# An FFN's operand rewritten with norm and shift from the third pair of tiles on, rows begun 64 bytes past 128, and a first modulation in five rounds

## The chip, the cores and the metric

The kernel runs on one core of a Trainium2 chip, as one launch. The metric is the device time of that launch in microseconds (us). All arithmetic is in float32; a product of two float32 operands is built from three matmuls in the rounded format float32r (the high parts with each other, and each high part with the other operand's low part).

## The reference

One step of a small diffusion backbone over 384 tokens of width 1024: 128 context tokens and 256 latent ones. There are two layers; each is half an FFN, a token mixer (latent attention, MLA, in layer 0; a state space model, SSM, in layer 1), and half an FFN.

```python
def adaln_input(x, g, shift, scale):
    return rmsnorm(x, g) * (1 + scale) + shift

def swiglu(h, w_in, w_out):
    gate, up = jnp.split(h @ w_in, 2, axis=-1)
    return (jax.nn.silu(gate) * up) @ w_out

def ffn_half(x, shift, scale, gate, g, w_in, w_out):
    return x + 0.5 * gate * swiglu(adaln_input(x, g, shift, scale), w_in, w_out)
```

Shift, scale and gate come from `silu(cond) @ mod_w + mod_b`, one set for context tokens and one for latent ones. `w_in` is 1024 x 5632, `w_out` 2816 x 1024. Every mixer, too, reads a normed and modulated x.

## The kernel before

Channels lie on the 128 partitions and tokens along the free axis. x is kept as `xT`, 8 rows of 384 tokens. The matmul operand is `xh` (high part) and `xl` (low part): x times scale and weight of the norm (`gs`), with two more columns, 384 and 385, that hold the shift of the two token groups. So a row has `NX` = 386 columns. The factor of the norm (one number per token) is not in it: it is found while the first matmuls run, spread over all partitions into `rext`, and multiplied into each result on its way out of PSUM, where the shift's column is added as a bias.

`wmm` takes the next 128 x 128 weight tile from a stream. Weights arrive as units of 8 tiles (512 KB) by `stream_dma`, four ahead; `stream_split` cuts a unit into `whi` (ScalarE, L109) and `wlo` (VectorE, L110), three ahead; a unit that is used up starts the split of the third next. Each `wmm` is three matmuls (L124, L125, L126: xh with wlo, xl with whi, xh with whi).

An FFN's first half computes 44 tiles of 128 outputs over 8 rows k: 22 pairs of a gate tile j and an up tile 22 + j, 1056 matmuls ("in" in the trace). `evac` turns a pair into the product, `ah` and `al`. The second half ("fo") multiplies these 22 rows with `w_out`, 8 tiles, 528 matmuls; `residual` adds each to x, writes the next operand's row (`prep_x`) and its square. `in_first_pair` starts the FFNs, MLA and SSM: 7 rows of two tiles, the norm's statistic (`norm_stat`) between them, and then row 7, which is written last. `Fill` spreads the modulation of later stages, VectorE sums over weight rows, over the matmuls of an FFN.

The first FFN has a head of its own, since its shift and scale must first be computed: in four rounds (`mod_round`), each of which gives two rows k. A round is a load of 2 MB in four pieces, 8 matmuls that sum over 1024 channels in four column groups (`psmod`, L141; the trace has two instructions for each), a copy, transposes, a reduction, and the rows of `xh` and `xl`. Between the rounds six tiles (`HEAD` = 3 pairs) take the rows that are ready.

The order of instructions on each engine is that of a list scheduler: what comes first in the program goes first, but an instruction that is not ready by the scheduler's own model of time lets later ones pass. Tiles of a pool lie one behind the other in the order in which they are first named, each begun on a multiple of 32 bytes.

## Time and profile before

| what | value |
|---|---|
| time, median of 3 runs | 1695.97 us (1695.53 to 1696.38) |
| profiled execution: time, span | 1695.77 us, 1694.0 us |
| busy: TensorE, VectorE, ScalarE, GpSimd | 1655.4, 1254.1, 791.7, 196.1 us |
| HBM traffic | 276.06 MB read, 4.28 MB written |

The span runs from the first instruction of the program to the last; the time has a little more around it. The profile calls TensorE's matmuls PE, its weight loads PEld, VectorE DVE, ScalarE ACT, GpSimd POOL, and the engine that issues most loads SP (SPq is its queue). Matmuls are pipelined: one begins before the one ahead has ended, so the time that one takes of the engine is the distance between starts and not its duration.

### The profile page before, as it was taken

What the parts mean: (1) busy time and instruction counts of PE and PEld (TensorE: products, weight loads), DVE (VectorE), ACT (ScalarE), POOL (GpSimd) and SP (SyncE); (2) the same over time, 40 slices, a digit from 0 to 9 for tenths busy, and PEclk for the clock granted to TensorE, in tenths of its full rate; (3) what the DMA queues carried; (4) which work ended last, traced back from release to release, by engine and by line L of the source; (5) the groups of instructions that cost most, each with busy time, mean ns of one, the idle gap of its engine ahead of it and who ended that gap; (6) DMA issues with size and microseconds to landing.
All of it is one profiled execution on the core that took longest, in us unless ns stands there. A gap on an engine that the chain in (4) does not pass through costs nothing.

```text
span 1694.0 us, 25203 instructions
## 1 busy us (share of the span) xinstructions
PE 1655.4 (98%) x9616; PEld 1584.6 (94%) x9631; DVE 1254.1 (74%) x2069; ACT 791.7 (47%) x1308; POOL 196.1 (12%) x180
## 2 busy tenths in 40 slices
PE   7999999999999999999999999999998999999996
PEld 3899999987899999999999999988897999999996
DVE  3798889579868888986888897888876765444443
ACT  3533333455544333334333333787766644333332
POOL 0111100110001111000111100023222201111000
PEclk9999999999999999999999999999998999999998
DMA  9476667443245666664666574354433333333331
GB/s 349 172 228 210 206 203 235 131 151 101 75 164 183 204 206 202 214 229 157 208 205 205 193 241 164 121 166 134 141 122 119 97 125 123 125 125 125 124 125 50
DMA packets 88441, 281.99 MB, mean 166 GB/s; under 512 B 9836, under 2 KB 19900, under 8 KB 87808
## 3 DMA queue, kind: packets, MB, share of 16 engines
q1 hardware_dynamic: 86560, 274.26, 49.6%
q0 software_dynamic: 1104, 5.28, 0.9%
q8 instruction: 75, 1.23, 0.3%
q10 hardware_dynamic: 656, 0.85, 0.1%
q14 instruction: 46, 0.38, 0.1%
HBM read 276.06 MB, written 4.28 MB: 165 GB/s over the span
## 4 chain that ended last, share of the span: by engine, by line
PE 88%; DVE 5%; ACT 4%; DMA 2%; issue 1%; SPq 0%; POOL 0%; DVEq 0%; ACTq 0%
PE in L124 17%; PE in L126 17%; PE in L125 17%; PE fo L124 7%; PE fo L126 7%; PE fo L125 7%; DVE ca L662 2%; DMA cp<-ecum_d 2%; PE so L124 1%; PE so L125 1%; PE so L126 1%; ACT L769 1%; PE psmod L141 1%; PE wo L124 1%; PE pv L548 1%
## 5 line engine op out<-in xcount | busy, mean ns | idle before, releaser
L124 PE MATMUL in<-xh,wlo 128*128 128x386 f32 x1792 | 613.0, 343 | 3.6 <-ACT xh L246 3.1
L109 ACT CAST whi<-raw 128x1024 fp32r<-128x1024 f32 x348 | 365.3, 1050 | 526.2 <-issue 227.0
L126 PE MATMUL in<-xh,whi 128*128 128x386 f32 x1792 | 610.1, 341 | 0.0
L125 PE MATMUL in<-xl,whi 128*128 128x386 f32 x1792 | 608.3, 339 | 0.2 <-DVE xl L248 0.2
L110 DVE TENSOR_TENSOR wlo<-raw,whi 128x1024 fp32r<-128x1024 f32 x348 | 430.5, 1237 | 129.9 <-ACT whi L109 129.6
L124 PEld LDWEIGHTS in<-xh,wlo 128*128 128x128 f32 x1792 | 339.2, 189 | 10.6 <-issue 4.5
L125 PEld LDWEIGHTS in<-xl,whi 128*128 128x128 f32 x1792 | 339.8, 190 | 4.9 <-issue 2.4
L126 PEld LDWEIGHTS in<-xh,whi 128*128 128x128 f32 x1792 | 337.9, 189 | 3.7 <-issue 3.7
L125 PE MATMUL fo<-al,whi 128*128 128x384 f32 x704 | 236.7, 336 | 0.0
L124 PE MATMUL fo<-ah,wlo 128*128 128x384 f32 x704 | 236.7, 336 | 0.0
L126 PE MATMUL fo<-ah,whi 128*128 128x384 f32 x704 | 236.7, 336 | 0.0
L183 DVE CUSTOM_DVE_ANT_0 work<-modraw,crow,cst 128x1024 f32<-128x1024 f32 x144 | 185.3, 1288 | 20.6 <-POOL al L327 19.3
L327 POOL TENSOR_TENSOR al<-work,ah 128x384 fp32r<-128x384 f32 x88 | 111.2, 1263 | 749.6 <-ACT ah L326 736.2
L124 PEld LDWEIGHTS fo<-ah,wlo 128*128 128x128 f32 x704 | 132.0, 187 | 0.0
L125 PEld LDWEIGHTS fo<-al,whi 128*128 128x128 f32 x704 | 132.0, 187 | 0.0
L126 PEld LDWEIGHTS fo<-ah,whi 128*128 128x128 f32 x704 | 132.0, 187 | 0.0
L183 DVE CUSTOM_DVE_ANT_0 workout<-modraw,crow,cst 128x1024 f32<-128x1024 f32 x96 | 123.1, 1282 | 6.5 <-DMA modraw<-in_modw_dram 5.0
L326 ACT CAST ah<-work 128x384 fp32r<-128x384 f32 x88 | 45.3, 514 | 131.0 <-DVE work L324 131.0
L319 DVE TENSOR_TENSOR work<-in,rext 128x386 f32<-128x386 f32 x88 | 49.1, 558 | 69.7 <-PE in L126 67.8
L320 DVE TENSOR_TENSOR work<-in,rext 128x386 f32<-128x386 f32 x88 | 48.8, 554 | 45.3 <-PE in L126 45.3
L322 ACT ACTIVATE work<-work 128x128 f32<-128x128 f32 (+1 forms) x176 | 70.6, 447 | 4.5 <-DVE work L319 4.1
L324 DVE SCALAR_TENSOR_TENSOR work<-work 128x128 f32<-128x128 f32 (+1 forms) x176 | 68.0, 427 | 5.2
(257 smaller groups left out, 1683.4 us busy)
## 6 DMA issues: line engine op xcount, KB each, us to landing
raw<-in_w_dram SPq DMA_DIRECT2D x348, 512.0 KB, 3.8
modraw<-in_modw_dram SPq DMA_DIRECT2D x128, 512.0 KB, 4.4
mod<-in_mod_dram SPq DMA_DIRECT2D x16, 512.0 KB, 9.9
cp<-ecum_d SPq DMA_DIRECT2D x32, 256.0 KB, 5.0
crow<-silu_d POOLq DMA_DIRECT2D x4, 1024.0 KB, 6.1
h<-in_h_dram SPq DMA_DIRECT2D x16, 128.0 KB, 3.4
out_dram<-sto SPq DMA_DIRECT2D x16, 128.0 KB, 2.3
xT<-in_xT_dram SPq DMA_DIRECT2D x4, 384.0 KB, 9.3
```

The lines of the kernel that those rows point to most:

```text
L109: nc.scalar.copy(his[u], raws[u])
L110: tt(out=los[u], in0=raws[u], in1=his[u], op=ALU.subtract)
L124: mm(out, wl, rh, start=start, stop=False)
L125: mm(out, wh, rl, start=False, stop=False)
L126: mm(out, wh, rh, start=False, stop=stop)
L183: nc.vector.tensor_tensor_reduce(out=junk(), in0=raw[n], in1=crow[:, s, :], scale=1.0, scalar=C("modb", j), op0=ALU.mult, op1=ALU.add, acc ...
L319: tt(out=g, in0=pg[:, :NX], in1=rext, op=ALU.mult)
L320: tt(out=u, in0=pu[:, :NX], in1=rext, op=ALU.mult)
L322: act(sg[:, a:b], g[:, a:b], AF.Silu, bias=g[:, NTOK + s:NTOK + s + 1])
L324: stt(out=sg[:, a:b], in0=u[:, a:b], scalar=u[:, NTOK + s:NTOK + s + 1], op0=ALU.add, in1=sg[:, a:b], op1=ALU.mult)
L326: nc.scalar.copy(ah[:, j, :], sg)
L327: nc.gpsimd.tensor_tensor(out=al[:, j, :], in0=sg, in1=ah[:, j, :], op=ALU.subtract)
```

## The change

There are four parts.

- **Operand written anew.** The first pairs of an FFN (two of them in `first_four`, three in the head of the first FFN) run as before on 386 columns, but row by row over all their tiles. Once `rext` is there, `normed_x` rewrites each row of `xh` and `xl` in place: t = x times gs times rext, xh = t + shift rounded, xl = t + shift - xh. From the third pair (in the first FFN the fourth) on, tiles read 384 columns, and `evac` is one Silu and one multiply. MLA and SSM keep the old way.
- **Rows.** A row of `xh` and `xl` is 416 floats apart (13 x 128 bytes), and `gs`, `pad`, `sel` and `rs` are placed or sized so that these rows, those of `ah` and `al` and MLA's operands begin 64 bytes past a multiple of 128.
- **Five rounds.** The first modulation comes in rounds of 1, 1, 2, 2 and 2 rows; all but the first round are loaded by one DMA each. Their places between head matmuls are written out anew.
- **Ahead of the first sums.** A Silu on a zeroed tile ahead of the constants' arrival, and five matmuls on zeros ahead of and between the sums of the first round.

```diff
+XROW = 416
+ROUNDS = ((0, 1), (1, 1), (2, 2), (4, 2), (6, 2))
...
+    gs = pers.tile([P, KT, 2], F32, tag="gs", name="gs")
+    xh = pers.tile([P, KT, XROW], F32R, tag="xh", name="xh")[:, :, 0:NX]
+    xl = pers.tile([P, KT, XROW], F32R, tag="xl", name="xl")[:, :, 0:NX]
-    xh = pers.tile([P, KT, NX], F32R, tag="xh", name="xh")
-    xl = pers.tile([P, KT, NX], F32R, tag="xl", name="xl")
+    rext = pers.tile([P, XROW], F32, tag="rext", name="rext")[:, 0:NX]
...
+    class FirstMod:
+        def __init__(self, pool, c32):
+            self.pool, self.c32, self.raw, self.sb = pool, c32, {}, {}
+
+        def load(self, r, parts):
+            k0, n = ROUNDS[r]
+            raw = self.raw[r] = self.pool.tile([P, KT, n, 2 * P], F32, tag=f"mod01_{r}", name=f"mod01_{r}")
+            src = mod01[:, k0 * KT * 2 * P:(k0 + n) * KT * 2 * P].rearrange("p (k x c) -> p k x c", k=KT, x=n)
+            h = KT // parts
+            for i in range(parts):
+                nc.sync.dma_start(raw[:, h * i:h * i + h], src[:, h * i:h * i + h])
+
+        def sums(self, r):
+            k0, n = ROUNDS[r]
+            raw, ps = self.raw.pop(r), bank(f"psmod_{r}")
+            for k in range(KT):
+                g = k % 4
+                mm(ps[32 * g:32 * g + 32, 0:2 * P * n], self.c32[:, k, :], raw[:, k].rearrange("p x c -> p (x c)"),
+                   start=(k < 4), stop=(k >= 4), tile_position=(0, 32 * g))
+            sb = self.sb[r] = self.pool.tile([P, 512], F32, tag="modsb", name=f"modsb_{r}", bufs=2)
+            nc.scalar.copy(sb[:, 0:2 * P * n], ps[:, 0:2 * P * n])
+
+        def prep(self, r):
+            k0, n = ROUNDS[r]
+            sb, pt, ks = self.sb.pop(r), bank("modT"), slice(k0, k0 + n)
+            for q in range(2 * n):
                 nc.tensor.transpose(pt[:, q * P:(q + 1) * P], sb[:, q * P:(q + 1) * P], T("ident"))
+            red = self.pool.tile([P, 2, 2, 2], F32, tag="modred", name=f"modred_{r}", bufs=2)
+            for c in range(2):
+                nc.vector.tensor_reduce(out=red[:, c, 0:n, :], in_=pt[:, 0:2 * P * n].rearrange(
+                    "p (x b g z) -> p b x z g", x=n, b=2, g=4)[:, c, :, 0:2, :], axis=AX.X, op=ALU.add)
+            m = mod[:, 0:2 * KT, :].rearrange("p (c k) s -> p c k s", c=2)[:, :, ks, :]
+            mb = C("modb", 0, 2 * KT).rearrange("p (c k) -> p c k", c=2)[:, :, ks]
+            tt(out=m, in0=red[:, :, 0:n, :], in1=mb.unsqueeze(3).to_broadcast([P, 2, n, 2]), op=ALU.add)
+            stt(out=gs[:, ks, :], in0=m[:, 1], scalar=1.0, op0=ALU.add,
+                in1=C("norm_g", k0, n).unsqueeze(2).to_broadcast([P, n, 2]), op1=ALU.mult)
             prep_shift(0, 0, ks)
+            for k in range(k0, k0 + n):
+                prep_x(k)
...
-        v, r, w = (pers.tile([P, 3], F32, tag=f"rs{i}", name=f"rs{i}", bufs=2) for i in range(3))
+        v, r, w = (pers.tile([P, 16], F32, tag=f"rs{i}", name=f"rs{i}", bufs=2)[:, 0:3] for i in range(3))
+        dg = pers.tile([P, NTOK], F32, tag="sq", name="dg", bufs=2)
...
+    def first_four(keyf, tiles, layer, sub):
+        ps = [bank(f"in{i}") for i in range(4)]
+        for k in range(KT):
+            for m, p in zip(tiles, ps):
+                wmm(p[:, :NX], keyf(m, k), xh[:, k, :], xl[:, k, :], k == 0, k == KT - 1)
+            if k == 1:
+                spread = norm_stat()
+            if k == 3:
+                spread()
+            if k >= 3:
+                for i in (range(4) if k == 3 else (k,)):
+                    normed_x(layer, sub, i)
+        return ps
+
+    def normed_x(layer, sub, k):
+        sh = sec(layer, 3 * sub)
+        t = pers.tile([P, NTOK], F32, tag="sq", name=f"xn{k}", bufs=2)
+        for s, a, b in SEGS:
+            stt(out=t[:, a:b], in0=xT[:, k, a:b], scalar=gs[:, k, s:s + 1], op0=ALU.mult, in1=rext[:, a:b], op1=ALU.mult)
+        for s, a, b in SEGS:
+            act(xh[:, k, a:b], t[:, a:b], AF.Identity, bias=sh[:, k, s:s + 1])
+        for s, a, b in SEGS:
+            stt(out=xl[:, k, a:b], in0=t[:, a:b], scalar=sh[:, k, s:s + 1], op0=ALU.add,
+                in1=xh[:, k, a:b], op1=ALU.subtract)
+
+    def in_tile(keyf, m, n=NX):
         ps = bank("in")
         for k in range(KT):
-            wmm(ps[:, :NX], keyf(m, k), xh[:, k, :], xl[:, k, :], k == 0, k == KT - 1)
+            wmm(ps[:, :n], keyf(m, k), xh[:, k, :n], xl[:, k, :n], k == 0, k == KT - 1)
         return ps
...
-    def head_mm(keyf, tiles, k0):
+    def head_mm(keyf, tiles, k):
         for m, ps in tiles:
-            for k in (k0, k0 + 1):
-                wmm(ps[:, :NX], keyf(m, k), xh[:, k, :], xl[:, k, :], k == 0, k == KT - 1)
+            wmm(ps[:, :NX], keyf(m, k), xh[:, k, :], xl[:, k, :], k == 0, k == KT - 1)
 
+            fp.tile([P, 16], F32, tag="pad", name="pad")
...
-            slots, skip = (2 * (NFF - HEAD) - 1, 0) if head is not None else (2 * NFF - 3, 4)
-            fill_in, fill_out = Fill(steps[:cut], slots, skip), Fill(steps[cut:], 4 * KT - 3)
+            first = HEAD if head is not None else 2
+            fill_in, fill_out = Fill(steps[:cut], 2 * (NFF - first) - 1), Fill(steps[cut:], 4 * KT - 3)
...
+            def product(j, sg):
+                nc.scalar.copy(ah[:, j, :], sg)
+                nc.gpsimd.tensor_tensor(out=al[:, j, :], in0=sg, in1=ah[:, j, :], op=ALU.subtract)
+
+            def scratch(j):
+                w = work[0] = fp.tile([P, 1024 + NTOK], F32, tag="work", name=f"work{j}", bufs=2)
+                return w[:, 1024:]
+
+            def evac_raw(j, pg, pu):
+                sg = scratch(j)
+                gu = fp.tile([P, 2, NX], F32, tag="gu", name=f"gu{j}", bufs=2)
+                g, u = gu[:, 0], gu[:, 1]
...
+                product(j, sg)
+
+            def evac(j, pg, pu):
+                sg = scratch(j)
+                act(sg, pg[:, :NTOK], AF.Silu)
+                tt(out=sg, in0=pu[:, :NTOK], in1=sg, op=ALU.mult)
+                product(j, sg)
 
             if head is not None:
-                head_mm(keyf, head[0:2], KT - 2)
-                spread = norm_stat()
-                head_mm(keyf, head[2:], KT - 2)
-                spread()
-                for j in range(HEAD):
-                    evac(j, head[2 * j][1], head[2 * j + 1][1])
-                first = HEAD
+                head_mm(keyf, head, KT - 1)
+                normed_x(layer, sub, KT - 1)
+                raw_tiles = [p for _, p in head]
             else:
-                pg0, pu0, spread = in_first_pair(keyf, 0, NFF)
-                first = 1
+                raw_tiles = first_four(keyf, (0, NFF, 1, NFF + 1), layer, sub)
+            for j in range(first):
+                evac_raw(j, *raw_tiles[2 * j:2 * j + 2])
             for j in range(first, NFF):
-                pg = in_tile(keyf, j)
+                pg = in_tile(keyf, j, NTOK)
                 fill_in()
-                if head is None and j == 1:
-                    spread()
-                pu = in_tile(keyf, NFF + j)
-                if head is None and j == 1:
-                    evac(0, pg0, pu0)
+                pu = in_tile(keyf, NFF + j, NTOK)
                 evac(j, pg, pu)
                 fill_in()
...
+        cst32 = sp0.tile([P, KT, 32], F32, tag="cst32", name="cst32")
+        nc.vector.memset(cst32, 0.0)
+
+        def load_x(a, b):
+            nc.sync.dma_start(xT[:, a:b, :], xT_d[:, a:b, :])
+
+        fm = FirstMod(sp0, cst32)
+        fm.load(0, 4)
         nc.sync.dma_start(tab[:, 0:256], tab_d[:, 0:256])
         stream_dma(0)
+        load_x(0, 1)
+        fm.load(1, 1)
         stream_dma(1)
+        load_x(1, 4)
+        fm.load(2, 1)
         stream_dma(2)
+        load_x(4, 8)
+        fm.load(3, 1)
         stream_dma(3)
+        fm.load(4, 1)
         crow = sp0.tile([2, 1024], F32, tag="crow2", name="crow2")
         nc.gpsimd.dma_start(crow, crow_d)
+        warm = sp0.tile([P, 256], F32, tag="warm", name="warm")
+        nc.vector.memset(warm, 0.0)
+        act(gs[:, 0, :], warm[:, 0:2], AF.Silu)
         act(cst32[:, :, 0:2], C("cc", 0, 16).rearrange("p (k s) -> p k s", s=2), AF.Silu)
         head = [(m + j, bank("in")) for j in range(HEAD) for m in (0, NFF)]
         key0 = ffn_key(0, 0)
+
+        def busy(n):
+            ps = bank("warm")
+            for i in range(n):
+                mm(ps[:, 0:256], warm[:, 0:P], warm, start=True, stop=True)
+
+        busy(4)
+        fm.sums(0)
         stream_split(0)
+        busy(1)
+        fm.prep(0)
+        stream_split(1)
+        for k in range(KT - 1):
+            if k == 0:
+                head_mm(key0, head[0:2], k)
+                fm.sums(1)
+                head_mm(key0, head[2:3], k)
+                fm.prep(1)
+                head_mm(key0, head[3:], k)
+                stream_split(2)
+            elif k in (1, 3, 5):
+                head_mm(key0, head[0:1], k)
+                fm.prep({1: 2, 3: 3, 5: 4}[k])
+                head_mm(key0, head[1:], k)
+            else:
+                head_mm(key0, head, k)
+            if k == 1:
+                act(crow, crow, AF.Silu)
+                nc.gpsimd.dma_start(silu_d, crow)
+            if k in (0, 2, 4):
+                fm.sums({0: 2, 2: 3, 4: 4}[k])
+            for i in ((k,) if k < 3 else (4, 5, 6, 7) if k == 3 else ()):
+                square(i, i == 0)
+            if k == 3:
+                square(3, False)
+            if k == 4:
+                spread = norm_stat()
+            if k == 5:
+                spread()
+                for i in range(5):
+                    normed_x(0, 0, i)
+            if k >= 5:
+                normed_x(0, 0, k)
```

In `FirstMod`, `raw` of rounds 1 to 4 is written by one DMA each; round 0 keeps four. In the other FFNs the head is replaced by `first_four`.

## Rows read from the trace of the kernel before

**Rows 1.** The page: busy time, share of the span and instructions of TensorE.
```profile
PE 1655.4 (98%) x9616; PEld 1584.6 (94%) x9631; DVE 1254.1 (74%) x2069; ACT 791.7 (47%) x1308; POOL 196.1 (12%) x180
```
**Rows 2.** The page: the chain that ended last, by engine.
```profile
PE 88%; DVE 5%; ACT 4%; DMA 2%; issue 1%; SPq 0%; POOL 0%; DVEq 0%; ACTq 0%
```
**Rows 3.** Stretches: length, busy time (instructions) of each engine, granted clock, DMA share, GB/s.
```profile
62.90:224.20 161.30, 161.30 (x913) 161.30 (x913) 143.73 (x226) 67.03 (x105) 27.07 (x21) 1.00 0.64 207
...
494.65:683.10 188.45, 188.45 (x1066) 188.00 (x1066) 154.48 (x244) 76.55 (x116) 25.02 (x21) 1.00 0.60 195
```
**Rows 4.** Order of time, TensorE, second FFN, "in": start, us; 720 matmuls apart.
```profile
540.19 0.34 PE L124 MATMUL in<-xh,wlo 128*128 128x386 f32 x1
...
667.59 0.34 PE L124 MATMUL in<-xh,wlo 128*128 128x386 f32 x1
```
**Rows 5.** Order of time, TensorE, "fo" of the same FFN; 360 matmuls apart.
```profile
700.28 0.34 PE L124 MATMUL fo<-ah,wlo 128*128 128x384 f32 x1
...
763.16 0.34 PE L124 MATMUL fo<-ah,wlo 128*128 128x384 f32 x1
```
**Rows 6.** Order of time, TensorE, the SSM's output "so"; 144 matmuls apart.
```profile
1365.06 0.33 PE L124 MATMUL so<-yhl,wlo 128*128 128x384 f32 x1
...
1390.02 0.33 PE L124 MATMUL so<-yhl,wlo 128*128 128x384 f32 x1
```
**Rows 7.** TensorE's groups by shape: count, busy us, mean ns of one, idle before.
```profile
L125 PE MATMUL so<-yl,whi 128*128 128x384 f32 x88 | 29.4, 334 | 0.0
...
L485 PE MATMUL v<-whi,ckvl 128*128 128x512 f32 x16 | 6.2, 388 | 0.0
```
**Rows 8.** Order of time, VectorE, from MLA's last rows to the FFN's third pair.
```profile
492.88 0.74 DVE L248 SCALAR_TENSOR_TENSOR xl<-xT,gs,xh 128x128 fp32r<-128x128 f32 x2
493.54 0.56 DVE L257 TENSOR_TENSOR acc<-acc,sq 128x384 f32<-128x384 f32 x1
...
499.27 0.16 DVE L218 TENSOR_SCALAR rs<-rs 128x3 f32<-128x3 f32 x1 [0.98 <-PE rs L216]
...
500.51 0.68 DVE L225 TENSOR_SCALAR dg<-tab,rs 128x128 f32<-128x128 f32 x3
...
510.69 0.55 DVE L319 TENSOR_TENSOR work<-in,rext 128x386 f32<-128x386 f32 x1
...
511.62 0.55 DVE L319 TENSOR_TENSOR work<-in,rext 128x386 f32<-128x386 f32 x1
512.09 0.34 DVE L324 SCALAR_TENSOR_TENSOR work<-work 128x128 f32<-128x128 f32 x1
```
**Rows 9.** The chain that ended last, in order of time: the norm's small matmuls.
```profile
498.54 0.69 PE rs L216 x6
...
508.38 0.64 PE rb L229 x2
```
**Rows 10.** Order of time, ScalarE, same stretch.
```profile
495.81 0.80 ACT L246 ACTIVATE xh<-xT,gs 128x128 fp32r<-128x128 f32 x2
...
509.42 0.47 ACT L230 COPY rext<-rb 128x384 f32<-128x384 f32 x1
```
**Rows 11.** VectorE's groups by line.
```profile
L110 DVE TENSOR_TENSOR wlo<-raw,whi 128x1024 fp32r<-128x1024 f32 x348 | 430.5, 1237 | 129.9 <-ACT whi L109 129.6
```
**Rows 12.** Stretches of the start, columns as in rows 3.
```profile
16.90:22.10 5.20, 5.13 (x13) 2.75 (x14) 2.93 (x6) 1.83 (x4) 0.00 (x0) 0.50 1.03 407
...
33.00:38.00 5.00, 5.00 (x25) 2.58 (x26) 0.00 (x0) 0.00 (x0) 0.00 (x0) 1.00 1.03 405
38.00:43.00 5.00, 5.00 (x27) 3.71 (x28) 2.60 (x12) 3.22 (x9) 0.00 (x0) 1.00 0.34 137
```
**Rows 13.** Order of time, TensorE, the start.
```profile
16.96 0.66 PE L124 MATMUL in<-xh,wlo 128*128 128x386 f32 x1 [3.08 <-ACT xh L246]
...
24.06 1.06 PE L141 MATMUL psmod<-mod,cst 128*32 128x512 f32 x8
...
31.39 1.05 PE L141 MATMUL psmod<-mod,cst 128*32 128x512 f32 x4
```

More of the change, by code (lines that the diff above doesn't have):

```diff
@@ L128, in wmm @@
             stream_used(u)
-    def mod_round(r, pool):
-        raw = pool.tile([P, KT, 512], F32, tag="mod01", name=f"mod01_{r}", bufs=4)
-        for i in range(4):
-            nc.sync.dma_start(raw[:, 2 * i:2 * i + 2, :], mod01[r][:, 2 * i:2 * i + 2, :])
-        def run():
-            ks = slice(2 * r, 2 * r + 2)
-            ps = bank(f"psmod_{r}")
-            for kt in range(KT):
-                g = kt % 4
-                mm(ps[32 * g:32 * g + 32, :], cst32[:, kt, :], raw[:, kt, :], start=(kt < 4), stop=(kt >= 4),
-                   tile_position=(0, 32 * g))
-            sb = pool.tile([P, 512], F32, tag="modsb", name=f"modsb_{r}", bufs=2)
-            nc.scalar.copy(sb, ps)
-            yield
-            pt = bank("modT")
-            for q in range(4):
-                nc.tensor.transpose(pt[:, q * P:(q + 1) * P], sb[:, q * P:(q + 1) * P], T("ident"))
-            red = pool.tile([P, 4, 2], F32, tag="modred", name=f"modred_{r}", bufs=2)
-            nc.vector.tensor_reduce(out=red, in_=pt.rearrange("p (b g z) -> p b z g", b=4, g=4)[:, :, 0:2, :],
-                                    axis=AX.X, op=ALU.add)
-            dst = mod[:, 0:2 * KT, :].rearrange("p (c k) s -> p c k s", c=2)
-            mb = C("modb", 0, 2 * KT).rearrange("p (c k) -> p c k", c=2)
-            for i in range(2):
-                tt(out=dst[:, :, ks, i], in0=red[:, :, i].rearrange("p (c k) -> p c k", c=2), in1=mb[:, :, ks], op=ALU.add)
-            prep_scale(0, 0, ks)
@@ L355, in ffn @@
                 ps = bank("fo")
-                work[0] = fp.tile([P, 1024 + 2 * NX + NTOK], F32, tag="work", name=f"workout{m}", bufs=2)
+                work[0] = fp.tile([P, 1024 + NTOK], F32, tag="work", name=f"workout{m}", bufs=2)
                 for k in range(NFF):
@@ L380, in lt @@
                 return lp.tile(shape, F32, tag=tag, name=tag, bufs=2)
+            mt([P, 16], "pad", 1)
             ckvh, ckvl = mt([P, 2, 512], "ckvh", 1, F32R), mt([P, 2, 512], "ckvl", 1, F32R)
@@ L954 @@
         key0 = ffn_key(0, 0)
-        next(runs[0])
-        act(crow, crow, AF.Silu)
-        nc.gpsimd.dma_start(silu_d, crow)
-        next(runs[0])
-        stream_split(0)
-        runs.append(mod_round(3, sp0))
-        load_x(3)
-        for u in (1, 2):
-            stream_split(u)
-        for r, c0, c1 in ((1, 1, 2), (2, 0, 1), (3, 0, 1)):
-            head_mm(key0, head[:c0], 2 * r - 2)
-            next(runs[r])
-            head_mm(key0, head[c0:c1], 2 * r - 2)
-            next(runs[r])
-            head_mm(key0, head[c1:], 2 * r - 2)
-            for kt in ((2 * r - 2, 2 * r - 1) if r < 3 else (4, 5, 6, 7)):
-                square(kt, kt == 0)
+        def busy(n):
[4 more added lines that the diff above has]
+        fm.sums(0)
+        stream_split(0)
+        busy(1)
[32 more added lines that the diff above has]
+                normed_x(0, 0, k)
     ffn(0, 0, (16, 40, 56), (0, 1), head)
```

30 lines of the change are left out of this document (4 added, 26 removed).

## The prediction

> **What bounds the kernel now.** I read the page's shares first, then the chain of waits, then stretches of the span, then single instructions. TensorE is busy for 1655.4 us, 98% of the 1694.0 us span [rows 1]; the chain that ended last runs 88% through TensorE, 5% through VectorE [rows 2]. So the spacing of matmuls, start to start, is the first thing to look at. In an FFN's first half TensorE is busy for the whole 188.45 us while VectorE is busy for 154.48 us of it; in the first FFN the 912 matmuls after the head fill 161.3 us without a hole [rows 3].
>
> Three spacings follow from first and last starts. In the first half ("in", 386 columns): 720 matmuls from 540.19 to 667.59 us, 127.40 / 720 = 176.94 ns [rows 4]. In the second half ("fo", 384 columns): 360 from 700.28 to 763.16, 62.88 / 360 = 174.67 ns [rows 5]. In the SSM's output ("so", also 384 columns): 144 from 1365.06 to 1390.02, 24.96 / 144 = 173.33 ns [rows 6]. The price of a column comes from two groups that differ in it: 512 columns last 388 ns, 384 last 334, so 54 / 128 = 0.42 ns [rows 7]. Two columns are 0.84 ns. They explain 0.84 of the 2.27 ns between "in" and "fo", and nothing of the 1.34 ns between "fo" and "so".
>
> What else differs is where rows begin. Adding up the tiles in order of allocation: rows of xh and xl are 1544 bytes apart, 12 x 128 + 8, so they begin at eight different places within 128 bytes; rows of ah and al begin on multiples of 128; rows of yh and yl ("so") begin 64 past one. The weights' chunks begin 64 past in all three. After the change xh, xl, ah and al begin 64 past, and the weights' chunks on multiples of 128, because the tiles ahead of them now add up to one.
>
> **The spacing, worked out.** Four FFNs have 1056 first-half matmuls each. 912 (first FFN) + 3 x 960 = 3792 drop to 384 columns; 144 + 3 x 96 = 432 keep 386. The change has no exact counterpart: moving rows 64 past with weights on a multiple. Bounds: 173.33 ns ("so", moving rows as after) and 174.67 ns ("fo", moving rows and weights half a 128 apart, as after). I take 173.33, because that is what moving rows 64 past have shown.
> At 173.33: 3792 x 3.61 = 13.7 us. The 432: to 173.33 + 0.84 = 174.17, 432 x 2.77 = 1.2. "fo": 2112 x 1.34 = 2.8. MLA and SSM first halves (168 + 984 matmuls, unchanged in columns): 3.2 us if all were on the path; I count 1.8, since the SSM's are partly behind other engines. MLA's q and wo, 384 matmuls rowed as "fo": 0.5. Together 20.0 us.
> At 174.67: 3792 x 2.27 = 8.6, the 432 at 175.5 give 0.6, MLA and SSM 0.9, "fo" nothing: 10.1 us.
> The Trainium skill (TensorE: Matmul & The Clock Gate, "Part 2: What happens when you issue a matmul") says that TensorE has separate read ports for the streamed operand and for the weights, so that loading weights takes nothing from a running matmul. By that rule the move of the weights costs nothing and the sum is the first one; no row here shows it either way.
>
> **The operand written anew.** In each FFN the first tiles use x times scale and the shift columns, as now; meanwhile the norm is found, and normed_x rewrites eight rows. Per row VectorE runs four scalar_tensor_tensor (one on 128 and one on 256 columns, twice), ScalarE two activations. A pair of the same kind is 0.74 us long, and the next instruction begins 0.66 us after it began [rows 8]; two pairs are 1.32 us a row, 10.6 us for eight. ScalarE's pair takes 0.80 us [rows 10], 6.4 for eight, beside VectorE. Weight splits go on: 1.24 us each [rows 11] (1.15 from start to start), one per 24 matmuls (4.2 us).
> Count from the first matmul of the FFN (three FFNs, first_four): 48 matmuls 8.4 us, the statistic's two groups of small matmuls, 0.69 and 0.64 us [rows 9], with the change-over about 1.5, and rext some 1.6 us after the second began (508.38 [rows 9], its copy ends at 509.89 [rows 10]). The small VectorE chain from 499.27 to the end of dg at 501.19 is 1.9 us [rows 8], and 24 matmuls (4.2 us) now lie over it, so TensorE does not wait there. At about 10.9 rext is ready; a split is then running, to 11.55. VectorE needs 10.6 + 2 x 1.15 and ends the eighth row at 24.4. TensorE has finished its 96 raw matmuls at 18.3 and wants row 8's xl at 22.2. Wait: 2.2 us; by the 0.74 for a pair it is 3.7. I take 3.0, three times 9.0. Against it: the norm's first matmul now stands behind 24 instead of 21 matmuls and so waits less for the last residual, some 0.8 us an FFN, -2.4.
> In the first FFN only 36 matmuls (6.3 us) of raw work lie behind the second group. Row 8 is wanted 10.8 us after it; VectorE has it after 1.85 + 10.6 + 2.3 = 14.8 to 17. I take 4.5 us. Sum +11.1 us. Behind the rows stand evac_raw and the modulation's fill; what waits for those is the bank of the first raw tile, wanted a full pair later (8.4 us), so they cost nothing unless the wait is twice as long.
>
> **Cheaper evacuation.** Per pair one activation and one multiply replace two multiplies with rext, two scalar_tensor_tensor and one activation. It frees over 1 us of VectorE per pair; I cost it at nothing, since matmuls run back to back over it [rows 3]. The gu, pad and rs tiles move addresses and no work; dg shares the two "sq" buffers, which only matters if a square is still in one.
>
> **The start.** Now the first head matmul starts at 16.96 us [rows 13], and the tile after the head at 62.9 [rows 3]. DMA runs at 1.03 of its engines until about 38 us and then falls to 0.34 while TensorE stays full [rows 12]: the loads are over, the head is not. Why: eight modulation instructions issued together, as at 24.06, take 1.06 us, but four also take 1.05, as at 31.39 [rows 13]. Loaded in four pieces, most of three rounds ran in fours: 4 x 1.05 us and the change-over, some 4.7 a round. In the change rounds 1 to 4 land whole, so two groups of eight, about 2.1 us a round, 1.2 for the half round. Work after the first matmul: 144 x 0.174 = 25.1, modulation 1.2 + 3 x 2.1 = 7.5, transposes 1.7, norm 1.5: 36 us. The first round is half as large (1 MB, some 2.6 us less at 405 GB/s [rows 12]) and the activation table is loaded before the constants arrive, so the first matmul should start near 13 us. The order, though, holds it: the second full round lands near 21, its rows are ready near 27; two pairs of rows follow at 6.3 us of matmuls, 2.1 of sums and 0.7 of transposes and seams, then the last pair, 6.3, and the norm's 1.5. That puts the tile after the head at 53.0, 9.9 us sooner. Bounds: 49 (last load near 36.5, sums, chain of 4, 36 matmuls with the norm) and 58.5 (fours again). The clock was at half (0.50, that is 1.2 GHz) from 16.9 to 22.1 [rows 12] after TensorE had idled before the first matmul; the dummy matmuls may spare about 2.5 us, which is inside these bounds.
>
> **Sum.** -20.0 + 11.1 - 9.9 = -18.8 us. The profiled execution took 1695.77 us, 1.77 beyond its span and 0.2 under the median of 1695.97; from the median: 1677.2 us.
>
> **Rivals.**
> - *A, the sum*: 1677, 0.48. Its own range 1668 to 1683.
> - *B, weights and moving rows half a 128 apart cost what "fo" shows*: -10.1 in place of -20.0, 1687, 0.27. For it: "fo" is that case and holds 174.67. Against: "fo" is also the case in which moving rows begin on a multiple.
> - *C, the start gains nothing*, because the order holds the sums back behind matmuls or because the pieces' place is taken by longer waits: 1687, 0.08.
> - *D, spacing goes by columns alone*: 3792 x 0.84 = 3.2 us, and nothing for the rest; 1696.0 - 3.2 - 9.9 + 11.1 = 1694, 0.07. Against it: "fo" and "so" differ at the same columns [rows 5, 6]. The Trainium skill (TensorE: Matmul & The Clock Gate, "Back-to-back issue gap") gives N / 2.4 + 2.5 ns, in which only columns count; by that rule 162.5 ns at 384, and the trace differs with 174.67 and 173.33.
> - *E, slower: VectorE takes the rows one after the other.* As normed_x is written, each row's last pair waits for ScalarE's 0.80 us. If VectorE's queue holds that order, a row is 0.66 + 0.80 + 0.66 + hand-overs, 2.3 us, eight are 18.6, and the waits are 10.2 in three FFNs and 12 in the first, +40 in place of +11: 1706. It decides once the waits pass 30 us, that is at about 2 us a row. Against it: the queue is not in written order now; the multiply of the next tile at 511.62 stands before the product of the last tile at 512.09, which waits for ScalarE [rows 8]. 0.10.
>
> **How the numbers follow.** Within 0.2% (3.4 us), about what a measurement of this kernel can tell from no change, lies D; above it E; A, B and C are faster: 0.83, 0.07, 0.10. The range from 1667 to 1691 holds A to C and leaves out D and E with the edges.
>
> **What would show it.** Right: "in" matmuls of 384 columns 173.3 to 173.4 ns apart, "fo" the same; a wait on VectorE's xl in the fifth tile of three FFNs of 2 to 4 us in all; modulation sums in eights; the tile after the head near 53 us. Wrong: spacing of 174.7 or more (B, D); waits on xl above 7 us an FFN, with t, xh, xl in strict turn (E); sums still in fours or the first matmul after 16 us (C). A half clock in the fifth tile, where matmuls come in drips of three, would add to the wait and stands in no term above.

## The result, and the profile after

The changed kernel takes 1681.32 us (median of 4 runs, 1680.57 to 1682.58) against 1696.12 (1695.53 to 1696.38): a ratio of 0.9914, 95% interval 0.9897 to 0.9931. It is 14.8 us faster where 18.8 were forecast; 1681.3 lies inside the likeliest case's own range. That the sum came out near does not make its terms right, and several were not. The profiled execution of after took 1682.58 us, its span 1680.7.

Going by the starts of each stage's first and last matmul (the seams of about 0.2 us between them are left out), the two profiled executions differ as follows.

| stage | before, us | after, us | difference |
|---|---|---|---|
| up to the first matmul of the tile after the head | 62.43 | 59.78 | -2.7 |
| rest of the first FFN's first half | 161.51 | 162.04 | +0.5 |
| first halves of the other three FFNs | 188.16, 188.20, 188.09 | 185.01, 184.88, 184.79 | -9.8 |
| four second halves ("fo") | 4 x 92.05 | 4 x 91.34 | -2.8 |
| MLA | 178.48 | 179.90 | +1.4 |
| SSM, and what follows the last "fo" matmul | 342.01 + 15.85 | 341.89 + 16.03 | +0.1 |
| span | 1694.0 | 1680.7 | -13.3 |

First the page: busy time, and the chain of waits.

```profile
PE 1640.8 (98%) x9642; PEld 1573.9 (94%) x9657; DVE 1230.7 (73%) x1962; ACT 784.5 (47%) x1296; POOL 211.8 (13%) x180
PE 83%; DVE 7%; ACT 4%; DMA 2%; issue 2%; POOL 0%; SPq 0%; DVEq 0%; ACTq 0%
```

TensorE bounds the kernel as it did [rows 1, 2], but VectorE has a little more of the chain. Order of time on TensorE, third FFN: first two matmuls of the first half, 720 apart, then two of "fo", 360 apart, then two of the SSM's output, 144 apart.

```profile
817.18 0.34 PE L123 MATMUL in<-xh,wlo 128*128 128x384 f32 x1
...
941.98 0.34 PE L123 MATMUL in<-xh,wlo 128*128 128x384 f32 x1
...
970.58 0.34 PE L123 MATMUL fo<-ah,wlo 128*128 128x384 f32 x1
...
1032.98 0.34 PE L123 MATMUL fo<-ah,wlo 128*128 128x384 f32 x1
...
1356.25 0.34 PE L125 MATMUL so<-yhl,whi 128*128 128x384 f32 x1
...
1381.41 0.34 PE L125 MATMUL so<-yhl,whi 128*128 128x384 f32 x1
```

"in" is 124.80 / 720 = 173.33 ns apart, where it was 176.94 [rows 4]; "fo" 62.40 / 360 = 173.33, where it was 174.67 [rows 5]; "so", whose columns and rows the change leaves as they were (only the weights' place moved), went up from 173.33 [rows 6] to 25.16 / 144 = 174.7.

Stretches of after: the first FFN's rest, the second FFN's first half, then two at half clock, one in the start and one in MLA (columns as in rows 3).

```profile
59.78:221.99 162.21, 160.24 (x913) 157.67 (x913) 140.15 (x197) 64.94 (x98) 29.02 (x21) 1.00 0.62 205
493.23:678.42 185.19, 185.19 (x1066) 184.29 (x1065) 151.41 (x220) 74.91 (x113) 30.09 (x21) 1.00 0.62 200
29.00:35.80 6.80, 6.13 (x19) 6.13 (x20) 4.70 (x10) 3.59 (x8) 0.00 (x0) 0.50 0.99 416
376.00:381.00 5.00, 4.80 (x19) 3.40 (x19) 3.07 (x9) 2.20 (x6) 0.00 (x0) 0.66 0.02 3
```

In the first FFN TensorE has holes now, 162.21 - 160.24 = 2.0 us, where there were none [rows 3]. MLA's stretch at 0.66 of the clock had 1.00 before. MLA's operations are untouched in all 14 profiled kernels of this document. In four of them the clock fell to half within MLA (this one, `e2_rows0`, `e9_both`, `e12_kick384`), and they took 179.9 to 180.2 us for it; the other ten took 178.2 to 178.5. So the 1.4 us came with the clock of this execution.

Order of time on TensorE in the start.

```profile
13.31 0.98 PE L123 MATMUL in<-xh,wlo 128*128 128x386 f32 x2 [3.05 <-DVE wlo L109]
...
24.43 1.92 PE L147 MATMUL psmod<-mod,cst 128*32 128x512 f32 x16
27.12 0.66 PE L156 MATMUL modT<-tab,modsb 128*128 128x128 f32 x4 [0.76 <-ACT modsb L150]
29.67 1.65 PE L123 MATMUL in<-xh,wlo 128*128 128x386 f32 x4 [1.89 <-ACT xh L254]
```

The head begins at 13.31 instead of 16.96 [rows 13], and sixteen modulation instructions take 1.92 us, so both of those steps hold. But between 26.35 and 29.67 TensorE has only four transposes, waits for the next rows, and then runs at half clock until 35.8 (4 matmuls in 1.65 us). The load was not what held these sums: in order of issue the queue had moved this round's last byte by about 20 us (an estimate from the bytes of the loads ahead of it), and TensorE was busy with row 1's matmuls until the sums began.

Two more views bear on the waits. The rows rewritten in the second FFN, on VectorE and then on TensorE:

```profile
515.75 1.14 DVE L301 SCALAR_TENSOR_TENSOR xn<-xT,gs,rext 128x256 f32<-128x256 f32 x3
516.80 1.40 DVE L305 SCALAR_TENSOR_TENSOR xl<-xn,mod,xh 128x128 fp32r<-128x128 f32 x4
```

```profile
515.42 0.51 PE L123 MATMUL in<-xh,wlo 128*128 128x384 f32 x2
...
517.00 0.56 PE L123 MATMUL in<-xh,wlo 128*128 128x384 f32 x2
```

VectorE writes two or more rows' parts in one go and ends the last xl at 518.20, which is 24.97 us after the FFN's first matmul at 493.23. On TensorE L123 comes twice in a row. We read this as the gate tile and the up tile of the pair going through the rows together, one xh with two wlo. Who TensorE waited for between 56 and 224 us:

```profile
PE in L123 <- DVE wlo L109: 1.2, 2, 0.7
PE in L124 <- DVE xl L305: 0.6, 2, 0.5
```

The larger of the two is not a rewritten row but a weight split.

### The profile page after: what moved, and what is told of

It reads as the page before. It is cut to its first block, busy times and chain, and to the rows that moved or that the text cites. A ratio compares the mean times of both kernels' runs of the same rounds, so it can differ in the third digit from the quotient of the medians.

```text
span 1680.7 us, 25083 instructions
## 1 busy us (share of the span) xinstructions
PE 1640.8 (98%) x9642; PEld 1573.9 (94%) x9657; DVE 1230.7 (73%) x1962; ACT 784.5 (47%) x1296; POOL 211.8 (13%) x180
## 4 chain that ended last, share of the span: by engine, by line
PE 83%; DVE 7%; ACT 4%; DMA 2%; issue 2%; POOL 0%; SPq 0%; DVEq 0%; ACTq 0%
PE in L123 16%; PE in L124 15%; PE in L125 15%; PE fo L124 7%; PE fo L123 7%; PE fo L125 7%; DVE ca L703 2%; PE so L123 1%; PE so L125 1%; PE so L124 1%; DVE wlo L109 1%; DMA cp<-ecum_d 1%; ACT L810 1%; DVE work L190 1%; DMA modraw<-in_modw_dram 1%
## 5 line engine op out<-in xcount | busy, mean ns | idle before, releaser
L123 PE MATMUL in<-xh,wlo 128*128 128x384 f32 (+1 forms) x1792 | 607.6, 341 | 8.0 <-DVE wlo L109 4.3
L124 PE MATMUL in<-xl,whi 128*128 128x384 f32 (+1 forms) x1792 | 606.4, 339 | 1.0 <-DVE xl L305 0.6
L125 PE MATMUL in<-xh,whi 128*128 128x384 f32 (+1 forms) x1792 | 604.6, 338 | 0.0
L109 DVE TENSOR_TENSOR wlo<-raw,whi 128x1024 fp32r<-128x1024 f32 x348 | 457.1, 1314 | 195.5 <-ACT whi L108 195.1
L123 PEld LDWEIGHTS in<-xh,wlo 128*128 128x128 f32 x1792 | 338.6, 190 | 15.9 <-ACT xh L254 3.9
L123 PE MATMUL fo<-ah,wlo 128*128 128x384 f32 x704 | 235.8, 335 | 0.0
L351 POOL TENSOR_TENSOR al<-work,ah 128x384 fp32r<-128x384 f32 x88 | 126.9, 1442 | 709.3 <-ACT ah L350 709.3
L190 DVE CUSTOM_DVE_ANT_0 work<-modraw,crow,cst 128x1024 f32<-128x1024 f32 x144 | 187.2, 1301 | 18.4 <-POOL al L351 16.8
L190 DVE CUSTOM_DVE_ANT_0 workout<-modraw,crow,cst 128x1024 f32<-128x1024 f32 x96 | 122.8, 1281 | 13.3 <-DMA modraw<-in_modw_dram 9.3
L123 PEld LDWEIGHTS fo<-ah,wlo 128*128 128x128 f32 x704 | 132.1, 188 | 0.0
L373 DVE TENSOR_TENSOR work<-in,work 128x384 f32<-128x384 f32 x79 | 43.9, 556 | 63.8 <-PE in L125 63.7
L254 ACT ACTIVATE xh<-xT,gs 128x128 fp32r<-128x128 f32 x96 | 41.1, 452 | 69.3 <-DVE xT L316 69.3
L703 DVE SCALAR_TENSOR_TENSOR ca<-u,cst,ca 128x386 f32<-128x386 f32 x96 | 70.2, 741 | 2.0 <-ACT ca L701 1.5
L316 DVE SCALAR_TENSOR_TENSOR xT<-fo,hg,xT 128x128 f32<-128x128 f32 x64 | 24.4, 412 | 31.4 <-PE fo L125 31.4
```

The costliest lines, as they stand in the source:

```text
L109: tt(out=los[u], in0=raws[u], in1=his[u], op=ALU.subtract)
L123: mm(out, wl, rh, start=start, stop=False)
L124: mm(out, wh, rl, start=False, stop=False)
L125: mm(out, wh, rh, start=False, stop=stop)
L190: nc.vector.tensor_tensor_reduce(out=junk(), in0=raw[n], in1=crow[:, s, :], scale=1.0, scalar=C("modb", j), op0=ALU.mult, op1=ALU.add, acc ...
L254: act(xh[:, kt, a:b], xT[:, kt, a:b], AF.Copy, scale=gs[:, kt, s:s + 1])
```

## The experiments

Each kernel is the changed one but for its edit. Before ran on the same chips at 1695.84 to 1695.91.

**Where weights and rows begin.** `e1_w64` puts the weights' buffers (and the small scratch tiles behind them) 64 bytes past a 128, like the moving rows. `e2_rows0` puts moving rows and weights both on multiples. `e3_scatter` spreads the rows of xh and xl over places as before the change.

```diff
 e1_w64
+    pers.tile([P, 16], F32, tag="padw", name="padw")        # behind rext
+    pers.tile([P, 16], F32, tag="padz", name="padz")        # behind rs
 e2_rows0
+    pers.tile([P, 16], F32, tag="padx", name="padx")        # behind gs
+    pers.tile([P, 16], F32, tag="padw", name="padw")        # behind rext
-            fp.tile([P, 16], F32, tag="pad", name="pad")
 e3_scatter
-XROW = 416
+XROW = 386
```

> The weights' buffers begin 64 bytes past a multiple of 128 as well as the moving rows; nothing else moves. Place theory (only where the moving rows begin decides): normed first halves 173.4 ns and second halves 173.3 ns as in the changed kernel, time within 1 us of 1681. Distance theory (what counts is the distance between moving rows and weights, as rival B has it): the distance is now 0 as it was in the SSM output before, and the second halves should leave the 173.3 that they have at a distance of 64, to about 174.7 (+3 us) or stay only by chance. If both stay at 173.3 the distance theory falls.

> Moving rows of the FFN (both halves) and weights all begin on multiples of 128. Place theory: second halves back to 174.7 ns (2112 matmuls, +2.8 us), normed first halves to about 174.7 (3792 matmuls, +4.9 us): 1689. Distance theory: 0 apart, like the SSM output of before, 173.3: 1681.

> Rows of the first half's operand are 1544 bytes apart again, so they begin at eight places; 384 columns in the normed tiles and everything else as changed. Place theory: normed first halves near 176.9 - 0.84 = 176.1 ns, +10 us: 1691. Columns theory (the two extra columns cost far more than 0.84 ns, and where rows begin little): they stay near 173.5 ns, within 2 us of 1681.

Measured: 1686.31 us (ratio 0.9946, 0.9932 to 0.9961), 1691.43 (0.9976, 0.9967 to 0.9985) and 1696.86 (1.0001, 0.9991 to 1.001). "in", 384 columns, 720 matmuls of the third FFN apart, in `e1_w64`, then in `e3_scatter`:

```profile
826.70 0.34 PE L126 MATMUL in<-xh,whi 128*128 128x384 f32 x1
...
953.10 0.34 PE L126 MATMUL in<-xh,whi 128*128 128x384 f32 x1
```

```profile
823.00 0.34 PE L123 MATMUL in<-xh,wlo 128*128 128x384 f32 x1
...
949.80 0.34 PE L123 MATMUL in<-xh,wlo 128*128 128x384 f32 x1
```

That is 126.40 / 720 = 175.56 ns (`e2_rows0` the same) and 126.80 / 720 = 176.11. At equal columns, places move "in" over 2.8 ns, and 64 bytes between moving rows and weights is the best of the four, not a penalty. "fo" kept 173.33 in `e1_w64`, and went to 176.0 in `e2_rows0` and 176.7 in `e3_scatter`. Neither theory of the expectations fits: with the weights moved "in" rose, which the place theory excludes, and "fo" did not, which the distance theory excludes. The value for `e3_scatter` is odd: no address of "fo" falls otherwise within 128 bytes there than in the changed kernel; the next experiments bear on it.

**Two columns.** `e4_c386` lets the normed tiles multiply 386 columns; two of them are computed and not read. All addresses stay. `e5_kick386` adds to it a matmul of one column ahead of each tile of "fo".

```diff
-                pg = in_tile(keyf, j, NTOK)
+                pg = in_tile(keyf, j)
...
-                pu = in_tile(keyf, NFF + j, NTOK)
+                pu = in_tile(keyf, NFF + j)
 e5_kick386, too
                 ps = bank("fo")
+                mm(bank("kick")[:, 0:1], T("ident"), T("ones")[:, 0:1], start=True, stop=True)
```

> The normed tiles are multiplied on 386 columns again (the two last ones are computed and not read); rows begin 64 past as changed. Place theory, 0.84 ns for two columns: 174.2 ns, +3.2 us: 1684. Columns theory: 176.7 ns like the unnormed tiles of the changed kernel, 3792 x 3.3 = +12.5 us: 1694.

> As the run with 386 columns in the normed tiles, where the second halves, with all addresses as in the changed kernel, kept 176.7 ns a matmul in place of 173.3; ahead of each of their 8 tiles now stands one more matmul of a single column (about 0.4 us with the change-over, 32 of them, +12 us if nothing else changes). Regime theory (a long row of equal matmuls keeps the spacing that it fell into at its start, and a disturbance lets it fall anew): some tiles of the second halves leave 176.7 for 174.7 or 173.3. Place theory: all stay at 176.7.

Measured: 1697.8 us (1.0016, 1.0006 to 1.0025) and 1700.92 (1.0028, 1.0016 to 1.004). In `e4_c386`, two of "in" 720 apart and two of "fo" 360 apart:

```profile
823.29 0.34 PE L123 MATMUL in<-xh,wlo 128*128 128x386 f32 x1
...
950.49 0.34 PE L123 MATMUL in<-xh,wlo 128*128 128x386 f32 x1
...
979.64 0.34 PE L123 MATMUL fo<-ah,wlo 128*128 128x384 f32 x1
...
1043.24 0.34 PE L123 MATMUL fo<-ah,wlo 128*128 128x384 f32 x1
```

Two columns cost 127.20 / 720 - 173.33 = 3.33 ns here, not 0.84. Columns and places do not simply add: with rows at eight places, 386 columns took 176.94 (before) and 384 took 176.11 (`e3_scatter`), which is 0.83 less; with rows 64 past, 176.67 and 173.33. So the places alone are worth 0.27 at 386 columns and the columns alone 0.83, but both together 3.61 (before's weights, too, lay 64 bytes elsewhere).

And "fo", whose columns, addresses and work are those of the changed kernel, stands at 63.60 / 360 = 176.67 from its first tile to its last. With the one-column matmuls the first tile stays at 176.7, and the other seven come to 174.67. So the spacing of "fo" is not a matter of its place alone: it takes over something from the matmuls before it, holds it for a whole stage, and small matmuls can change it. The time still rose, since each added matmul opens a gap: 312 ns from the last matmul of a tile to the first of the next.

**The same matmul in the changed kernel.** `e12_kick384` is the changed kernel with that one line ahead of "fo".

> The changed kernel with a matmul of one column ahead of each tile of the second half (fo). Addresses as in the changed kernel. If the spacing is a state that small matmuls reset, fo goes from 173.3 to the 174.65 ns that the same matmuls brought in the kernel with 386 columns (fo stage 93.1 us instead of 91.34, total 1688 us). If the state brought from the first half lasts through, fo stays at 173.3 ns and only the added matmuls count (some 92.4 us, 1685.7 us).

Measured: 1689.15 us, one run. Two matmuls of one tile of "fo", 60 apart:

```profile
969.70 0.34 PE L124 MATMUL fo<-al,whi 128*128 128x384 f32 x1
...
980.18 0.34 PE L124 MATMUL fo<-al,whi 128*128 128x384 f32 x1
```

10.48 / 60 = 174.67, in all eight tiles: the value that the same line brought from 176.67, now reached from 173.33. What "fo" does is a state, and this line sets it, from either side. (The added matmul also takes a bank of PSUM in the rotation, so that "fo" falls into others; that part was not tested by itself.) The stage takes 93.69 us in place of 91.34, a little more than either expectation.

**No rewriting at all.** `e10_rawall` leaves out `normed_x`; every pair multiplies 386 columns and goes through rext, as before the change. Start, addresses and the first four tiles' order stay.

```diff
-                    normed_x(layer, sub, i)          # and in the head
-                pg = in_tile(keyf, j, NTOK)
+                pg = in_tile(keyf, j)
-                evac(j, pg, pu)
+                evac_raw(j, pg, pu)                  # and the up tile's NTOK
```

> The changed kernel without normed_x: every pair of tiles multiplies 386 columns of x times scale and is evacuated with rext, as before the change; start, addresses and the first four tiles' order stay. If the rewritten rows make TensorE wait only 4 us in all, as the trace of the changed kernel shows, the time is that of the kernel with rewritten rows and 386 columns (1697.8) less 4: 1694 us. If they cost the 11 us of the prediction: 1687 us.

Measured: 1692.79 us (0.9984, 0.9975 to 0.9993). Second FFN, from the fifth tile, and its "fo":

```profile
508.15:677.75 169.60, 169.60 (x962) 169.60 (x962) 143.92 (x226) 68.05 (x106) 23.23 (x21) 1.00 0.63 199
677.75:771.03 93.28, 93.28 (x530) 93.28 (x530) 77.42 (x122) 32.42 (x45) 2.09 (x2) 1.00 0.66 216
```

No wait is left on TensorE, "in" and "fo" stand at 176.67 (169.60 / 960 and 93.28 / 528). Rewriting is worth 1692.8 - 1681.3 = 11.5 us: 3792 x 3.34 = 12.7 in "in", 4 x (93.10 - 91.34) = 7.0 in "fo", less the waits of 5.4 us (worked out below). The profiled spans differ by 10.0 only, since in the changed kernel's the clock fell in the start and in MLA: its tile after the head comes 2.5 us later, its MLA takes 1.4 more. The time lies nearer to the first expectation's 1694 than to 1687.

**A little more VectorE per row.** `e11_rows3` issues the longer xl instruction twice.

```diff
+            if s == 1:
+                stt(out=xl[:, k, a:b], in0=t[:, a:b], scalar=sh[:, k, s:s + 1], op0=ALU.add,
+                    in1=xh[:, k, a:b], op1=ALU.subtract)
```

> The changed kernel with the longer of the two xl instructions of each rewritten row issued twice (the second writes the same numbers). That is 0.39 us more of VectorE a row, 3.1 us by the eighth. If the rows are now just in time (in the second FFN the last is ready 0.6 us ahead of its matmul), TensorE waits for most of it: some 2.5 us in each of four FFNs, 1691 us. If TensorE has other work to cover it: 1681 to 1683 us.

Measured: 1689.28 us (0.9963, 0.9949 to 0.9977). From the fifth tile on the three later FFNs take 171.2, 169.7 and 168.7 us where the changed kernel takes 166.6 to 166.8, the first FFN 165.1 instead of 162.0: 12.7 us, more than the 10 expected. (The time rose by 8.0 only: in this profiled execution the clock held after the start's wait, below, and in MLA.) Who TensorE waited for in the second FFN's first half:

```profile
PE in L123 <- DVE wlo L109: 2.5, 2, 2.2
```

And the stretch behind the longer of these waits:

```profile
525.75:529.16 3.41, 3.41 (x11) 3.41 (x12) 3.41 (x3) 1.62 (x3) 1.24 (x2) 0.50 0.65 172
```

So the clock fell to half there. The third FFN has the same waits (2.4 us) and no such stretch, and lost 3.1 us where the second lost 4.5; 1.4 us of the 12.7 are therefore the clock's and not a wait. The prediction names such a half clock and has no term for it.

What is late is again a weight split, pushed back behind the rows in VectorE's queue. So the rows are just in time; there is no cover beyond a microsecond.

**The clock in the start.** `e6_busy` issues five dummy matmuls (ten instructions) where TensorE waits for the rows of the third round, the first that brings two rows; the prediction and the expectations call it the second full one.

```diff
                 fm.prep({1: 2, 3: 3, 5: 4}[k])
+                if k == 1:
+                    busy(5)
```

> Five more matmuls on zeros (1.8 us) behind the transposes of the third round, where TensorE now idles from 27.8 to 29.7 us before row 2. Clock theory: the half clock that follows from 29.0 to 35.8 us comes from this idle time; with it filled, row 2's 18 matmuls take 0.18 instead of 0.32 us, the tile after the head starts near 57 us in place of 59.8, time 1678.5. Chain theory: what holds the head is the chain of copy, transposes, reduction and rows; the tile after the head stays at 59.8 or later.

Measured: 1678.23 us (0.9894, 0.9879 to 0.9909). The same wait and what follows it in `e6_busy`, then in `e12_kick384`, which has no dummies:

```profile
26.50:28.70 2.20, 2.20 (x13) 1.87 (x11) 1.75 (x8) 1.39 (x6) 0.00 (x0) 1.00 1.00 417
28.70:35.50 6.80, 6.80 (x45) 4.94 (x43) 4.07 (x8) 2.94 (x6) 0.00 (x0) 1.00 0.99 416
```

```profile
24.00:28.50 4.50, 2.53 (x21) 0.78 (x20) 1.75 (x7) 1.69 (x5) 0.00 (x0) 1.00 0.97 409
28.50:35.50 7.00, 6.32 (x43) 5.12 (x43) 4.71 (x10) 3.61 (x8) 0.00 (x0) 1.00 1.01 425
```

With dummies the clock holds at 1.00 and the tile after the head starts at 56.04 instead of 59.78. But it held without them too: of the ten profiled kernels with this start and these loads and no dummies, three (`e10_rawall`, `e11_rows3`, `e12_kick384`) show 1.00 after the wait and seven show half clock. These three ran on another chip than the six of the seven whose chip is on record; on the chip of `e6_busy` the clock fell in both kernels without dummies (`e5_kick386`, `e7_al_dve`). That the dummies prevent it is likely and not shown.

The price can be read from the first matmul of row 2 (29.67 in the changed kernel) to the tile after the head. It is 27.3 to 27.4 us where the clock held, with dummies or without; 28.9 to 29.0 where it was at half for 3.4 us (`e3_scatter`, `e4_c386`, `e5_kick386`); 30.1 to 30.2 where it was for 6.8 us (the changed kernel, `e1_w64`, `e2_rows0`, `e7_al_dve`). So it costs the changed kernel 2.8 us. Its half clock at the first matmuls, 6.8 us long where others have 3.4, costs about 1 more, ahead of row 2. The median is 3.1 us lower with the dummies, but the intervals of the two kernels overlap.

**Al on VectorE.** In the first FFN's rest 19 of 38 weight splits overlap GpSimd's subtraction for al; those last 1737 ns on average, the other 19 1222. `e7_al_dve` moves the subtraction to VectorE.

```diff
-                nc.gpsimd.tensor_tensor(out=al[:, j, :], in0=sg, in1=ah[:, j, :], op=ALU.subtract)
+                tt(out=al[:, j, :], in0=sg, in1=ah[:, j, :], op=ALU.subtract)
```

> The subtraction that makes al runs on VectorE instead of GpSimd in all four FFNs. Contention theory (the weight split takes 2.04 us instead of 1.22 while GpSimd subtracts, and in the first FFN TensorE waits some 2 us for late splits): all splits at 1.22 us, no wait on wlo after the head in the first FFN, 1679. Load theory (VectorE simply has too much to do there): 22 x 0.55 us more on VectorE make the waits in the first FFN longer, 1683 or more.

Measured: 1678.72 us (0.9894, 0.9878 to 0.9911). Splits between 62 and 222 us (least, median, most ns), changed kernel, then `e7_al_dve`:

```profile
L109 DVE TENSOR_TENSOR wlo<-raw,whi x38: 1209/1226/2094, 61.2 to 219.2; 128x1024 fp32r<-128x1024 f32 x38
```

```profile
L109 DVE TENSOR_TENSOR wlo<-raw,whi x38: 1215/1223/1227, 62.6 to 219.2; 128x1024 fp32r<-128x1024 f32 x38
```

No split is slowed any more, and the first FFN's rest takes 160.63 us instead of 162.04: 1.4 of the 2.6 us of the medians. In `e9_both`, below, it takes 160.63 again, while the kernels with al on GpSimd and the same spacings (the changed one, `e6_busy`, `e8_pieces`, `e12_kick384`) take 161.8 to 162.7. The rest of the gain is within the runs' spread, and the intervals of the two kernels' times overlap. The Trainium skill (SBUF — State Buffer, "Who interferes with whom") says that a VectorE instruction with two SBUF inputs contends with a GpSimd instruction that reads SBUF; the splits have two such inputs, the subtraction reads SBUF, and the trace agrees (1737 ns against 1222).

**Loads in four pieces.** `e8_pieces` loads rounds 1 to 4 in four DMAs each, as before the change.

```diff
-        fm.load(1, 1)
+        fm.load(1, 4)                                # and rounds 2 to 4
```

> Rounds 1 to 4 of the first modulation are loaded in four pieces each, as all rounds were before; order otherwise as changed. By the prediction's step (sums run in eights only when a round lands whole): sums come in fours again, each round about 2.6 us longer on TensorE, the tile after the head 6 to 8 us later, 1688. Rival: the first pieces land sooner, so sums start sooner and fill idle time of TensorE; the tile after the head at 60 or earlier, 1681 or less.

Measured: 1690.47 us (0.9967, 0.9954 to 0.998). Modulation instructions on TensorE:

```profile
25.66 1.05 PE L147 MATMUL psmod<-mod,cst 128*32 128x512 f32 x4
...
27.55 1.05 PE L147 MATMUL psmod<-mod,cst 128*32 128x512 f32 x4
```

Fours are back, at 1.05 us each, and the tile after the head starts at 67.23, 7.5 us later than in the changed kernel and 4.8 later than before the change. The step is right, and for the head the expected size, 6 to 8 us; the time rose by 9.1 us where some 7 were expected. The loads are a little slower, too: between 19 and 24 us the pieces move 417 GB/s, whole rounds 426, and the first head matmul comes at 15.73 where the kernels with whole rounds have it at 13.1 to 14.5. And the clock fell once more in this head, from 56.2 to 59.6 us.

**Both repairs.** `e9_both` joins `e6_busy` and `e7_al_dve`.

> The changed kernel with five dummy matmuls after the second full modulation round's transposes and with al's subtraction on VectorE, that is both repairs together. If the two losses are separate (the clock in the head, the weight splits slowed by GpSimd in the first FFN), their gains add: 1681.3 - 3.1 - 2.6 = 1675.6 us. If both only shorten the same wait, one of them is all there is: about 1678 us.

Measured: 1677.07 us (0.989, 0.9876 to 0.9903), the fastest kernel here. The head ends at 57.07, the first FFN's rest takes 160.63, as in `e7_al_dve`. It lies between the two expectations, and its interval does not part it from either repair alone.

This kernel differs from `e7_al_dve` by its dummies in the start alone (the two ran on different chips). Two matmuls of MLA's "wo", 120 apart, some 440 us later, in `e7_al_dve`, then in `e9_both`:

```profile
468.78 0.34 PE L123 MATMUL wo<-oh,wlo 128*128 128x384 f32 x1
...
489.74 0.34 PE L123 MATMUL wo<-oh,wlo 128*128 128x384 f32 x1
```

```profile
466.29 0.34 PE L123 MATMUL wo<-oh,wlo 128*128 128x384 f32 x1
...
487.09 0.34 PE L123 MATMUL wo<-oh,wlo 128*128 128x384 f32 x1
```

That is 20.96 / 120 = 174.67 ns and 20.80 / 120 = 173.33, with the same MLA. "so", too, stands at 173.3 in `e2_rows0`, where its rows and weights begin at the same places within 128 bytes as in the changed kernel, which has 174.7. So a stage's pace can differ though neither it nor the stage ahead was edited. "fo" is steadier: in all six kernels where "in" ran at 173.33 and no matmul was added ahead of it, it ran at 173.33 in all four FFNs. But each kernel was profiled once, and the times of `e3_scatter` and `e4_c386` spread over 5 to 6 us, so another execution may have other spacings.

## Why the prediction came out, step by step

- **Spacing of the normed tiles** (13.7 us by 173.33): right, 173.33. The reason given, that "so" has shown it for rows 64 past, was only part: it takes the columns, the rows' places and the weights' place together (`e4_c386`, `e3_scatter`, `e1_w64`), and "so" itself left 173.33 with neither its columns nor its rows changed. That the value borrowed from it fitted is in part luck. Rival B's price is excluded: weights and rows half a 128 apart ran at 173.33, and nothing apart they ran slower (`e1_w64`). The rule of the Trainium skill that was weighed there (TensorE: Matmul & The Clock Gate, "Part 2: What happens when you issue a matmul") would make the weights' place cost nothing; with it moved, "in" went from 173.33 to 175.56, and "fo" did not move.
- **The price of a column.** A step that failed: 0.84 ns for two columns, from durations [rows 7], taken to hold at any place. With scattered rows it does (0.83); with rows 64 past it is 3.33 ns (`e4_c386`). Therefore the raw tiles, MLA's and the SSM's first halves, which keep 386 columns, did not come to 174.17; they stand near 176.5, and the 1.2, 1.8 and 0.5 us booked for them and for MLA's q and wo did not come, save for some tenths. Rival D, columns alone, has the same price and fell because places and columns came together.
- **"fo"** (2.8 us): the size is exact, the reason is not. It was booked on the rows' new place; at that same place it is 173.33, 174.67 or 176.67, by what ran before (`e4_c386`, `e10_rawall`, `e12_kick384`). Had the normed tiles kept 386 columns, "fo" would have lost 4.2 us.
- **Waits for rewritten rows** (11.1 us): sized at twice what came. `e10_rawall` has no waits; its times, scaled from 176.67 to 173.33, are what the changed kernel would take without any. Against them the first FFN's rest has 4.1 us of waits; `e7_al_dve`, without slowed splits, keeps 2.7 of them, the rows' share (4.5 priced). The other three FFNs have 1.3 in all (9.0 priced). The 2.4 us credited to the norm's earlier place, and 0.8 for spacing, should show in these FFNs' first four tiles; they took 18.2 to 18.3 us instead of 18.4 to 18.5, 0.6 us in all. VectorE was forecast well: the eighth row at 24.4, measured 24.97. The failing step is "wants row 8's xl at 22.2": that took the fifth and sixth tile one after the other, while the scheduler runs them row by row together, and by the count of matmuls the eighth row's turn comes at 25.9. `e11_rows3` shows how near that is. Rival E fell: rows overlap.
- **What the sum lacked:** slowed weight splits in the first FFN, 1.4 us, from GpSimd beside VectorE (`e7_al_dve` gives them back).
- **The start** (9.9 us): first matmul near 13 (13.31), sums in eights, right. The 9.9 itself was read 0.5 too large: the tile after the head began at 62.43 before the change, and 62.9 is only where the stretch of [rows 3] was begun. It now came at 59.8, not 53.0. The steps that failed: "its rows are ready near 27", where they came at 29.67, since their sums began only at 24.43, behind row 1's matmuls (2.7 us, of which about 1 is the long half clock at the first matmuls); the three pairs of rows from there on, booked at 26.0, which take 27.3 to 27.4 even at full clock (1.3); and the clock, which the prediction had met at the first matmuls only [rows 12] and set aside as "inside these bounds": at half again after this wait it cost 2.8. 53.0 + 2.7 + 1.3 + 2.8 is 59.8. Rival C's reason, sums held back behind matmuls, was therefore at work, at a part of its price.

So spacing gave about 3 us less than booked, the start 7 less, and waits cost 6 less; MLA's stretch of half clock took another 1.4 in the profiled execution. Errors of opposite sign left 4 us: that the sum came so near is luck.

## What to carry to other kernels

Price a narrower operand by the spacing of matmuls at that width and at the places that its rows will have, not by the difference of two durations; and undo one part at a time before crediting a stage's gain to what was edited in it, since a stage can inherit its pace. Before counting a wait, read from the trace whether the scheduler lets neighbouring tiles share the rows. A wait of TensorE may cost more than its length, when the clock falls behind it.

## What the runs showed that was not expected

- The same 528 matmuls at the same addresses run 173.33, 174.67 or 176.67 ns apart, constant over a stage of some 92 us, by what preceded them; a matmul of one column ahead of a tile moves them to 174.67. Why is open: nothing in the trace distinguishes them but the spacing.
- Two columns less and rows begun 64 bytes past a 128 gave 0.83 and 0.27 ns each alone, and 3.61 together.
- 64 bytes more or less under the weights' buffers cost 2.2 ns a matmul in "in" and nothing in "fo".
- A weight split lasts 1222 ns alone and up to 2094 beside a GpSimd subtraction.
- After the same wait in the start the clock was at half in seven profiled executions and full in three; 6.8 us at half cost 2.8 us.
